# Another order of steps in the first stage of a transformer layer

## The chip, the cores and the metric

The kernel runs on one core of a Trainium2 chip, in one launch. The metric is the time of one execution on the device, in microseconds (us), lower is better. Five engines run at once, each through its own queue and strictly in that queue's order: TensorE (PE: matrix products; PEld is its weight load), VectorE (DVE), ScalarE (ACT), GpSimd (POOL) and SyncE (SP, which issues most transfers).

## The reference

One layer of an encoder in float32, for 256 tokens of width 2048. `c` is one vector that modulates all tokens.

```
c_act = silu(c)
mod = c_act @ mod_w + mod_b                        # 2048 -> 6 x 2048
sh_m, sc_m, g_m, sh_f, sc_f, g_f = split(mod, 6)
h = x * (1 + sc_m) + sh_m
q, k, v = split(h @ w_qkv + b_qkv)                 # 2048 -> 3072
q, k = rope(q), rope(k)                            # sin and cos of the positions
y = softmax with a sink(q k^T / 8, |q - k| <= 128) v @ w_o + b_o
x = layer_norm(alpha * x + (1 + g_m) * y)
h = x * (1 + sc_f) + sh_f
y = square(relu(h @ w1 + b1)) @ w2 + b2            # 2048 -> 8192 -> 2048
out = layer_norm(alpha * x + (1 + g_f) * y)
```

## The kernel before, in words

**Precision.** Each float32 operand of the large products is split into a high part (`hh`, `wh`) and a low part (`hl`, `wl`), and three TensorE products are summed: high by high (line 542), high by low (543), low by high (544). So each block of weights of 1 MB, once it has landed in a buffer `raw`, needs two casts on ScalarE (`wh`, line 281) and two subtractions on VectorE (`wl`, line 252, "lows" below).

**Stream.** All weights pass through one queue in a planned order (`S.plan`, `Stream`). A block is loaded as soon as one of the eight `raw` buffers of the first stage is free; a buffer comes free when the block's last reader has been recorded. `S.vecs(n)` performs the next n steps of modulation in that queue; the casts of the next block of weights can stand only behind the steps that are planned ahead of it.

**Modulation.** `mod` is cut by feature tiles k of 128 features (16 of them). For each k of the mixer's scale and shift there are two blocks of 1 MB. They are reduced either on TensorE (`Mod.step`, line 336, 32 pieces in the profile for one block, then the copy `mrow` at line 365 and a small product at line 416 that turns the row into columns), or on VectorE (`Col.step`, line 376, a product with `cb` summed along the row; `cb` is the activated vector spread over all partitions by `spread()`, line 137). `MIXP` says for each k which way: 1 is TensorE. `Group.columns` adds the bias, and `modulated(k)` makes `hh` (ScalarE, line 570) and `hl` (VectorE, lines 571 and 572) of the input tile.

**First stage.** The loop over n from 0 to 11 (line 650) takes one block of `wqkv` each, which holds four units (k, p): feature tile k against column part p of three. A unit is 12 matmuls: two token tiles by three products, each of them two. `AHEAD[n]` names the tiles whose blocks are planned behind block n and whose steps are made in its time; the strings `steps` give the order of units (`u`), steps of modulation (`g`) and `modulated` (`m`). TensorE's sums stay in six banks over all 12 blocks; the bias is added by line 197, the sums are copied out at line 581. `idle(n)` runs n products without use ahead of the first data. `bias_rows` prepares the bias, `rotary_tables` the sines and cosines, `masks` the window.

**After it.** The rest of the queries' and values' products runs between the attention of one group and the next (`SLOT_FILL` says how many steps of modulation are planned in each slot), then the output product, the first layer norm (`norm_scalars`, `normed`), and the MLP. The modulation ahead of the MLP comes in four groups of four tiles (`m_ff`): `FFP` says how many tiles of each group go to TensorE.

**Order.** What a scheduler does not pin stands where it puts it; casts, lows, `modulated` and the first product of a step of modulation keep the order of the program.

## Time and profile before

| | us |
|---|---|
| median of 3 runs (lowest, highest) | 1129.77 (1128.59, 1130.95) |
| profiled execution: time | 1130.56 |
| profiled execution: span of the core | 1128.8 |
| TensorE busy | 1072.6 |
| VectorE busy | 766.7 |
| ScalarE busy | 526.9 |

The profiled execution's time is 1.76 us more than the span, for what lies around it. Busy times are sums over the whole span; stages with different limits are mixed in them. PEclk in the views is the clock granted to TensorE as a share of full speed. In a row of the timeline the brackets hold the idle time of the engine ahead of that instruction and who ended it.

### The profile page before, as it was taken

The numbers are of one execution on the slowest core, as the hardware profiler recorded it, in microseconds if no ns is written. First come the engines' busy times: TensorE is split into PE (matmuls) and PEld (weight loads), VectorE is DVE, ScalarE is ACT, GpSimd is POOL, SyncE is SP. The second block draws the span as 40 slices with busy tenths as digits, with TensorE's granted clock in tenths as the row PEclk, the third lists the DMA queues.
The fourth block names the chain that finished last, engine by engine and source line by source line (L and its number), as shares of the span: only waits on it lengthen the run. The fifth ranks groups of instructions, "written<-read, shape, count | busy, mean of one in ns | idle before, by whom it ended". The sixth has DMA issues, their size and how long they took to land.

```text
span 1128.8 us, 16294 instructions
## 1 busy us (share of the span) xinstructions
PE 1072.6 (95%) x6563; PEld 887.9 (79%) x6563; DVE 766.7 (68%) x1103; ACT 526.9 (47%) x814; POOL 20.4 (2%) x40
## 2 busy tenths in 40 slices
PE   7778799999999699999999999999999999999995
PEld 6566577777778599998888888888888888888884
DVE  2656687877679866765568787865665656665576
ACT  3332357777753445653344443344444334444340
POOL 1000000000000000000000001000000000000001
PEclk9988899999999899999999999999999999999998
DMA  9989988877798878555587877776555555557521
GB/s 384 426 358 425 359 295 330 298 278 271 248 390 305 333 259 313 183 187 192 199 304 272 296 261 273 294 295 223 185 187 189 198 201 194 186 188 261 187 75 74
DMA packets 43653, 292.75 MB, mean 259 GB/s; under 512 B 4877, under 2 KB 5037, under 8 KB 9785
## 3 DMA queue, kind: packets, MB, share of 16 engines
q1 hardware_dynamic: 40400, 281.96, 67.7%
q0 software_dynamic: 2432, 8.41, 2.3%
q10 hardware_dynamic: 744, 1.34, 0.3%
q8 instruction: 51, 0.84, 0.3%
q14 instruction: 26, 0.20, 0.0%
HBM read 289.57 MB, written 2.11 MB: 258 GB/s over the span
## 4 chain that ended last, share of the span: by engine, by line
PE 86%; DVE 9%; ACT 3%; issue 1%; DMA 1%; DVEq 0%; ACTq 0%
PE pa L1046 16%; PE pa L543 15%; PE pa L544 15%; PE pa L542 15%; PE pa L1047 8%; DVE raw L376 4%; PE pm L336 4%; PE pa L1022 3%; PE pa L1023 3%; PE pa L1024 3%; DVE wl L252 3%; PE pa L715 1%; PE pt L754 1%; PE pa L770 1%; ACT wh L281 1%
## 5 line engine op out<-in xcount | busy, mean ns | idle before, releaser
L252 DVE TENSOR_TENSOR wl<-raw,wh 128x1024 fp32r<-128x1024 f32 x332 | 403.8, 1223 | 233.1 <-ACT wh L281 230.2
L281 ACT CAST wh<-raw 128x1024 fp32r<-128x1024 f32 x332 | 346.8, 1051 | 414.2 <-PE pa L544 214.6
L543 PE MATMUL pa<-wl,g 128*128 128x512 f32 x816 | 323.4, 396 | 22.0 <-DVE wl L252 21.9
L542 PE MATMUL pa<-wh,g 128*128 128x512 f32 x816 | 319.3, 397 | 4.9 <-ACT wh L281 4.0
L544 PE MATMUL pa<-wh,g 128*128 128x512 f32 x816 | 321.1, 394 | 0.0
L1046 PE MATMUL pa<-g,wh 128*128 128x512 f32 x768 | 271.6, 399 | 0.0
L1047 PE MATMUL pa<-g,wl 128*128 128x256 f32 x768 | 215.7, 281 | 0.0
L543 PEld LDWEIGHTS pa<-wl,g 128*128 128x128 f32 x816 | 155.3, 190 | 57.6 <-DVE wl L252 25.5
L542 PEld LDWEIGHTS pa<-wh,g 128*128 128x128 f32 x816 | 152.9, 188 | 45.1 <-issue 7.5
L544 PEld LDWEIGHTS pa<-wh,g 128*128 128x128 f32 x816 | 155.2, 190 | 33.0 <-issue 0.6
L1046 PEld LDWEIGHTS pa<-g,wh 128*128 128x128 f32 x768 | 144.3, 188 | 36.2 <-issue 0.2
L1047 PEld LDWEIGHTS pa<-g,wl 128*128 128x128 f32 x768 | 145.1, 189 | 0.1
L376 DVE CUSTOM_DVE_ANT_0 raw<-raw,cb 128x2048 f32<-128x2048 f32 x54 | 122.9, 2286 | 15.4 <-DMA raw<-in_mod 15.3
L1022 PE MATMUL pa<-g,wh 128*128 128x256 f32 x256 | 74.3, 290 | 0.3 <-ACT g L958 0.3
L1023 PE MATMUL pa<-g,wh 128*128 128x256 f32 x256 | 73.2, 287 | 0.0
L1024 PE MATMUL pa<-g,wl 128*128 128x256 f32 x256 | 72.8, 285 | 0.0
L1022 PEld LDWEIGHTS pa<-g,wh 128*128 128x128 f32 x256 | 49.8, 195 | 2.1 <-ACT g L958 1.1
L1023 PEld LDWEIGHTS pa<-g,wh 128*128 128x128 f32 x256 | 49.8, 195 | 0.4 <-issue 0.4
L1024 PEld LDWEIGHTS pa<-g,wl 128*128 128x128 f32 x256 | 49.7, 194 | 0.0
L336 PE MATMUL pm<-raw,cact 128*32 128x128 f32 (+1 forms) x1216 | 48.9, 305 | 0.0
L336 PEld LDWEIGHTS pm<-raw,cact 128*32 128x32 f32 x1216 | 34.2, 117 | 14.7 <-issue 12.1
L732 ACT ACTIVATE g<-g,nm 128x256 f32<-128x256 f32 x64 | 31.9, 500 | 18.6 <-DVE nm L722 18.6
(180 smaller groups left out, 659.0 us busy)
## 6 DMA issues: line engine op xcount, KB each, us to landing
raw<-in_mod SPq DMA_DIRECT2D x96, 1024.0 KB, 7.2
raw<-in_w SPq DMA_DIRECT2D x64, 1024.0 KB, 4.9
raw<-in_w1b SPq DMA_DIRECT2D x48, 1024.0 KB, 4.9
raw<-in_wqkv SPq DMA_DIRECT2D x24, 1024.0 KB, 7.1
raw<-in_wo SPq DMA_DIRECT2D x16, 1024.0 KB, 6.8
raw<-in_w1a SPq DMA_DIRECT2D x16, 1024.0 KB, 7.3
g<-in_x SPq DMA_DIRECT2D x4, 512.0 KB, 7.4
gb<-in_lnrow POOLq DMA_DIRECT2D x8, 256.0 KB, 6.0
```

Source lines behind the costliest of these rows:

```text
L252: self.pinned(nc.vector.tensor_sub(l, r, f32(self.hs[n])))
L281: self.pinned(nc.scalar.copy(h, s))
L336: i = nc.tensor.matmul(self.ps[32 * j:32 * j + 32, :w], lhsT[j] if type(lhsT) is list else lhsT, rhs[j], start=self.first, stop=stop)
L376: S.pinned(nc.vector.tensor_tensor_reduce(out=raw, in0=raw, in1=cb, scale=1.0, scalar=0.0, op0=OP.mult, op1=OP.add, accum_out=self.dst))
L542: nc.tensor.matmul(ps, xh, wh, start=start, stop=False)
L543: nc.tensor.matmul(ps, xh, wl, start=False, stop=False)
L544: S.prev = nc.tensor.matmul(ps, xl, wh, start=False, stop=stop).ins
L1022: nc.tensor.matmul(o, wh(w, 128), hh, start=new, stop=False)
L1023: nc.tensor.matmul(o, wh(w, 128), hl, start=False, stop=False)
L1024: nc.tensor.matmul(o, wl(w, 128), hh, start=False, stop=end)
L1046: nc.tensor.matmul(ps, wh(k, 128), hb, start=k == 0, stop=False)
L1047: nc.tensor.matmul(ps[:, :256], wl(k, 128), hb[:, :256], start=False, stop=k == NK - 1)
```

## The change

What it does, in the order of the program:

- The vector `c` gets a transfer of its own on SP (8 KB), and the packed constants move to ScalarE's queue, ahead of the first input tile.
- `spread()` and `bias_rows` move from ahead of the loop to behind its first turn; `idle(8)` becomes `idle(20)` ahead of the first step of modulation, and the five between the first two steps become six.
- `MIXP`: feature tiles 4, 8 and 12 go to VectorE and the other 13 to TensorE (before: 9 on TensorE, 7 on VectorE).
- `AHEAD` is written out by hand; tile 2 moves from the first turn to the second. In `steps` each `g` is now one block (before two), with units between; a tile that is left over at the end of a turn is modulated behind the first unit of the next (`owed`).
- `rotary_tables` becomes a generator: its five parts are made one per turn from n = 3 to 7 (before all in turn 2).
- `FFP`: the first MLP group goes to VectorE whole, the second to TensorE whole (before two tiles of each group to either). `columns` gets a form for four tiles.
- The activation `warm` (a square root without use) reads the last softmax sums in place of a constant.

```
-MIXP = tuple(int(k < 3 or k % 2 == 0) for k in range(16))
+MIXP = tuple(int(k not in (4, 8, 12)) for k in range(16))
-FFP = (2, 2, 2, 2)
+FFP = (0, 4, 2, 2)
...
+    cT = cst.tile([128, NK], F32, name="cT")
+    nc.sync.dma_start(cT, a["cT"])
     pack = cst.tile([128, 274], F32, name="pack")
-    nc.sync.dma_start(pack, a["pack"])
+    nc.scalar.dma_start(pack, a["pack"])
...
+            elif p == 2:
                 nc.tensor.transpose(pt[:, :128], r[:, :128], ident)
...
+            else:
+                for h in range(2):
+                    nc.tensor.transpose(pt[:, h * 128:h * 128 + 128], r[:, h * 128:h * 128 + 128], ident)
...
-    AHEAD, nm = [], 1
+    AHEAD = [[1], [2, 3], [4, 5], [6], [7], [8, 9], [10], [11], [12, 13], [14], [15], []]
...
     load_x(0)
-    bq = bias_rows(a["bqkv"], QKV)
-    spread()
-    idle(8)
     S.pin = True
+    idle(20)
     S.vecs(1)
-    idle(5)
+    idle(6)
     S.vecs(1)
     modulated(0)
     idle(6)
...
+    owed, tables = [], rotary_tables()
     for n in range(12):
         u, ms = units(n), list(AHEAD[n])
-        steps = "uuugmugm" if n == 0 else ["uuuu", "ugumuu", "ugumugum"][len(ms)]
-        for x in steps:
+        if n == 1:
+            steps = "ugugmugug"
+        else:
+            steps = ["uuuu", "ugugumu", "ugugumgug"][len(ms)]
+        for i, x in enumerate(steps):
             if x == "u":
                 next(u)
             elif x == "g":
-                S.vecs(2)
+                S.vecs(1)
             else:
                 modulated(ms.pop(0))
+            if i == 0 and owed:
+                modulated(owed.pop())
+        owed = ms
+        if n == 0:
+            spread()
+            bq = bias_rows(a["bqkv"], QKV)
         if n == 1:
             msk = masks()
-        if n == 2:
-            trig = rotary_tables()
+        if 3 <= n < 8:
+            next(tables)
...
-            warm = sml.tile([128, 1], F32, name="warm")
-            nc.scalar.activation(warm, eps, AF.Sqrt)
+            warm = sml.tile([128, 4], F32, name="warm")
+            nc.scalar.activation(warm, sums_of[0], AF.Sqrt)
```

**How the instructions move: the start on TensorE.** In the rows below, a line is one group of equal instructions in TensorE's queue; `identr` is the idle product, `raw,cact` a block of modulation, `ident,cact` the spreading of `cb`, `both,mrow` the turn of a row into columns. TensorE's first rows, before:

```order
L1213 UNCONDITIONAL_BRANCH
L137 MATMUL pa<-ident,cact 128x128 x16
L635 MATMUL pa<-identr 128x512 x8
L336 MATMUL pm<-raw,cact 32x128 x16
L635 MATMUL pa<-identr 128x512 x5
```

TensorE's first rows, now:

```order
L1236 UNCONDITIONAL_BRANCH
L647 MATMUL pa<-identr 128x512 x20
L343 MATMUL pm<-raw,cact 32x128 x16
L647 MATMUL pa<-identr 128x512 x6
L343 MATMUL pm<-raw,cact 32x128 x16
L423 MATMUL pt<-both,mrow 128x2
```

The 16 products that spread `cb` no longer stand at the head; they now stand in three groups around the last unit of the first turn and the first of the second.

**The middle of the first stage on VectorE.** `raw,cb` is a block of modulation on VectorE (tiles 7 before and 12 now), `wl<-raw,wh` a low. VectorE's rows, before:

```order
L376 ISA raw,modm<-raw,cb 128x2048
L376 ISA modm 128x1
L252 TENSOR_TENSOR wl<-raw,wh 128x1024
L410 TENSOR_TENSOR modm<-modm,pack 128x2
L571 TENSOR_SCALAR g_507<-g_507,modm 128x256
L572 TENSOR_TENSOR g_728<-g_507,g_727 128x256
```

VectorE's rows, now:

```order
L259 TENSOR_TENSOR wl<-raw,wh 128x1024 x2
L436 TENSOR_TENSOR modm<-pt,pack 128x2
L583 TENSOR_SCALAR g_562<-g_562,modm 128x256
L584 TENSOR_TENSOR g_777<-g_562,g_776 128x256
L259 TENSOR_TENSOR wl<-raw,wh 128x1024 x2
L383 ISA raw,modm<-raw,cb 128x2048
L383 ISA modm 128x1
```

A block on VectorE now stands behind both lows of the block of weights at hand, where before the lows stood behind the block. On ScalarE, in the same place, `g<-g,modm` is line 570 (now 582). Before:

```order
L365 COPY mrow<-pm 128x128
L570 ACTIVATE g_727<-g_507,modm 128x256
L281 CAST wh<-raw 128x1024 x2
L570 ACTIVATE g_727<-g_507,modm 128x256
L365 COPY mrow<-pm 128x128
```

ScalarE, now:

```order
L372 COPY mrow<-pm 128x128
L582 ACTIVATE g_776<-g_562,modm 128x256
L288 CAST wh<-raw 128x1024 x2
L372 COPY mrow<-pm 128x128
L582 ACTIVATE g_776<-g_562,modm 128x256
```

In most turns the two casts of the next block now stand right behind the modulation of a tile that came through TensorE.

**The first layer norm.** `sd` is the root of the variance of one of the two token tiles, `g<-g,nmr,r` the normalising of the second one. ScalarE, before:

```order
L789 ACT_TABLE_LOAD
L789 ACTIVATE sd<-ve 128x1
L281 CAST wh<-raw 128x1024
L789 ACTIVATE sd<-ve 128x1
L281 CAST wh<-raw 128x1024
L808 ACTIVATE g_2391<-g_2391,nmr,r_3360 128x512
```

ScalarE, now:

```order
L812 ACT_TABLE_LOAD
L812 ACTIVATE sd<-ve 128x1 x2
L288 CAST wh<-raw 128x1024 x2
L831 ACTIVATE g_2500<-g_2500,nmr,r_3448 128x512
L831 ACTIVATE g_2502<-g_2502,nmr,r_3448 128x512
```

VectorE at the same place, before (`qq` and `r` are steps of the reciprocal root):

```order
L794 TENSOR_SCALAR qq<-qq 128x1
L252 TENSOR_TENSOR wl<-raw,wh 128x1024
L795 TENSOR_TENSOR r_3360<-r_3360,qq 128x1
L252 TENSOR_TENSOR wl<-raw,wh 128x1024
L805 SCALAR_TENSOR_TENSOR nmr<-mv,r_3360 128x1
```

VectorE, now:

```order
L817 TENSOR_SCALAR qq<-qq 128x1
L833 TENSOR_SCALAR g_2506<-g_2506,mv,r_3407 128x512
L818 TENSOR_TENSOR r_3448<-r_3448,qq 128x1
L259 TENSOR_TENSOR wl<-raw,wh 128x1024
L828 SCALAR_TENSOR_TENSOR nmr<-mv,r_3448 128x1
L259 TENSOR_TENSOR wl<-raw,wh 128x1024
```

Both roots now stand ahead of the two casts; before one cast stood between them. Ahead of `nmr` stood two lows, now one.

More of the change, by code (lines that the diff above doesn't have):

```diff
@@ L101, in f32 @@
         return x.bitcast(F32)
+    cT = cst.tile([128, NK], F32, name="cT")
+    nc.sync.dma_start(cT, a["cT"])
     pack = cst.tile([128, 274], F32, name="pack")
-    nc.sync.dma_start(pack, a["pack"])
-    cT, b1 = pack[:, :NK], pack[:, NK:NK + 64]
+    nc.scalar.dma_start(pack, a["pack"])
+    b1 = pack[:, NK:NK + 64]
     modmb, modfb, gateb, lnT = (pack[:, 80 + 32 * n:112 + 32 * n].rearrange("p (n k) -> p n k", n=2)
@@ L148, in masks @@
         return msk
+    trig = cst.tile([128, 2, 3, NT, 32], F32, name="trig")
     def rotary_tables():
@@ L163, in rotary_tables @@
         nc.vector.tensor_scalar_add(kk, kk, -magic)
+        yield
         for cc in (c1, c2, c3):
@@ L167, in rotary_tables @@
         nc.vector.tensor_scalar(ang, ang, pi, -pi, op0=OP.min, op1=OP.max)
-        trig = cst.tile([128, 2, 3, NT, 32], F32, name="trig")
-        nc.scalar.activation(trig[:, 0, 2], ang, AF.Sin)
+        yield
         nc.vector.tensor_scalar_mul(nang, ang, -1.0)
@@ L173, in rotary_tables @@
         nc.vector.tensor_scalar_add(nang, nang, float(np.float32(math.pi / 2)))
+        yield
+        nc.scalar.activation(trig[:, 0, 2], ang, AF.Sin)
         nc.scalar.activation(trig[:, 0, 0], nang, AF.Sin)
+        yield
         nc.vector.tensor_scalar_mul(trig[:, 0, 1], trig[:, 0, 2], -1.0)
         nc.vector.tensor_scalar_mul(trig[:, 1], trig[:, 0], DH ** -0.5)
-        return trig
+        yield
     def bias_rows(src, n):
@@ L417, in columns @@
                 v = pt[:, :2].rearrange("p (n k) -> p n k", n=2)
-            else:
+            elif p == 2:
                 nc.tensor.transpose(pt[:, :128], r[:, :128], ident)
                 v = pt[:, :128].rearrange("p (n k q) -> p n k q", n=2, k=2)[:, :, :, 0]
+            else:
+                for h in range(2):
+                    nc.tensor.transpose(pt[:, h * 128:h * 128 + 128], r[:, h * 128:h * 128 + 128], ident)
+                v = pt[:, :256].rearrange("p (h j q) -> p j h q", h=2, j=4)[:, :, :, 0]
+                for n in range(2):
+                    d, b = (u[:, n, k0:k0 + 4].rearrange("p (j h) -> p j h", j=2) for u in (self.dst, self.mb))
+                    nc.vector.tensor_tensor(d, v[:, 2 * n:2 * n + 2], b, op=OP.add)
+                return
             nc.vector.tensor_tensor(self.dst[:, :, k0:k0 + p], v, self.mb[:, :, k0:k0 + p], op=OP.add)
@@ L483, in hybrid_kernel @@
         S.plan(a["wqkv"][n])
-        top = min((4 * n + 7) // 3, NK - 1)
-        AHEAD.append(list(range(nm, top + 1)))
-        for k in AHEAD[-1]:
+        for k in AHEAD[n]:
             if k in (2, 4, 8, 12):
@@ L489, in hybrid_kernel @@
             m_mix[k].plan(2)
-        nm = top + 1
     late = [m_gm] + m_ff[:3]
@@ L735, in scores @@
         PS[n] = P, sm, es
+    sums_of = []
     def normalise(n):
         P, sm, es = PS.pop(n)
+        sums_of[:] = [sm]
         rs = sml.tile([128, 4], F32, name="rs")
@@ L1195, in _layout @@
     o["lnrow"] = cc(np.stack([gm, bm, f(i["ln_mlp_g"])[0], f(i["ln_mlp_b"])[0]]))
-    flat = [o.pop(n).reshape(128, -1) for n in ("cT", "b1", "modmb", "modfb", "gateb", "lnT")]
+    flat = [o[n].reshape(128, -1) for n in ("cT", "b1", "modmb", "modfb", "gateb", "lnT")]
     snk = f(i["attn_sink"])[0].reshape(4, 2, 2, 2).transpose(0, 2, 1, 3).reshape(NH)
```

## The prediction

> **What bounds the kernel now.** I read the groups of instructions first, then the busy time of each engine by stage, then what TensorE waited for in the first stage.

> ```profile
> L252 DVE TENSOR_TENSOR wl<-raw,wh 128x1024 fp32r<-128x1024 f32 x332 | 403.8, 1223 | 233.1 <-ACT wh L281 230.2
> L376 DVE CUSTOM_DVE_ANT_0 raw<-raw,cb 128x2048 f32<-128x2048 f32 x54 | 122.9, 2286 | 15.4 <-DMA raw<-in_mod 15.3
> ```

> A low costs VectorE 1.22 us, and its idle time is spent on casts of ScalarE. A block of modulation on VectorE costs 2.29, nearly two lows. By stage (window, its length, then busy time of PE, PEld, DVE, ACT and POOL, then granted clock, DMA share, GB/s):

> ```profile
> 19.00:145.40 126.40, 99.75 (x824) 74.89 (x824) 77.13 (x112) 38.14 (x56) 0.00 (x0) 0.88 0.97 394
> 145.40:353.00 207.60, 205.42 (x1414) 152.86 (x1414) 163.74 (x317) 141.09 (x320) 3.87 (x7) 1.00 0.82 305
> 392.00:1128.80 736.80, 724.13 (x3997) 624.43 (x3997) 488.30 (x604) 326.04 (x412) 11.51 (x17) 0.99 0.62 219
> ```

> From 145.4 on TensorE is busy for 98% of these windows and has nothing to give. In the first stage 26.65 us of 126.4 are idle on TensorE, and the clock is 0.88. DMA is busy at 0.97, but only because `raw` buffers are refilled as they come free; who is waited for is told by TensorE's waits from 17 to 146 us (total, times, longest):

> ```profile
> PE pa L543 <- DVE wl L252: 21.1, 6, 5.8
> PE pa L542 <- ACT wh L281: 4.0, 3, 1.8
> PE pt L416 <- ACT mrow L365: 1.4, 3, 0.5
> PE pa L542 <- ACT g L570: 0.9, 1, 0.9
> ```

> Six waits for lows carry 21.1 us. One of them, and what follows a short idle time on the clock:

> ```profile
> 68.83 0.80 PE L543 MATMUL pa<-wl,g 128*128 128x512 f32 x1 [5.82 <-DVE wl L252]
> ```

> ```profile
> 34.00:38.00 4.00, 4.00 (x12) 3.05 (x12) 4.00 (x5) 2.05 (x3) 0.00 (x0) 0.57 1.01 428
> ```

> The lows of those blocks stand in VectorE's queue behind one or two blocks of modulation. The first stage is thus bounded by VectorE's order, not by VectorE's total (77 of 126 us) nor by the transfers.

> **The change part by part: TensorE's start.** The rows of before from the first instruction to the first main product, and VectorE's bias casts:

> ```profile
> 4.67 6.51 PE L137 MATMUL pa<-ident,cact 128*128 128x128 f32 x32 [4.67 <-ACT cact L126]
> 10.93 2.09 PE L635 MATMUL pa<-identr 128*128 128x512 f32 x8
> 12.96 1.08 PE L336 MATMUL pm<-raw,cact 128*32 128x128 f32 x32
> 19.06 1.68 PE L542 MATMUL pa<-wh,g 128*128 128x512 f32 x6 [0.35 <-ACT wh L281]
> ```

> ```profile
> 7.50 0.43 DVE L192 CAST g<-g 128x512 fp32r<-128x512 f32 x1 [1.77 <-DMA g<-in_bqkv]
> 8.09 0.68 DVE L193 TENSOR_TENSOR g<-g,g 6x512 fp32r<-6x512 f32 x1
> ```

> The spreading (6.51) and eight idle products (2.09) go from the head; 20 idle products take their place. At 0.26 each (2.09/8) they take 5.2 us, at twice that 10.4; begun at about 4.67 they end between 9.9 and 15.1. Before, the first block began at 12.96. I take no change there, since the idle products are likely half cold, half warm. Behind it one more idle product: +0.23. The first main product then starts at 19.06 + 0.23 = 19.3 (bounds 17 and 21.4). The transfer of `c` on its own is small and ahead of all else on SP; `pack` is first needed by the bias behind the first small product, some 4 us after the first block: nothing, bounds -0.5 to +0.5, in the range.

> **TensorE's work in the stage.** The pace, from the chain that ended last and the timeline in the middle of the stage:

> ```profile
> 20.97 0.23 PE pa L544
> 30.73 0.27 ACT mrow L365
> 31.05 0.40 PE pt L416 x2
> 31.66 0.60 ACT g L570
> 32.26 0.94 ACT wh L281
> 33.23 0.98 DVE wl L252
> ```

> ```profile
> 111.90 1.08 PE L336 MATMUL pm<-raw,cact 128*32 128x128 f32 x32
> 112.91 0.50 PE L543 MATMUL pa<-wl,g 128*128 128x512 f32 x1
> 113.24 0.40 PE L544 MATMUL pa<-wh,g 128*128 128x512 f32 x1
> 113.48 0.32 PE L416 MATMUL pt<-both,mrow 128*128 128x2 f32 x2
> 115.62 0.80 PE L542 MATMUL pa<-wh,g 128*128 128x512 f32 x2 [1.82 <-ACT wh L281]
> 144.84 0.61 PE L197 MATMUL pa<-g,g 128*128 128x512 f32 x2
> 145.39 1.07 PE L336 MATMUL pm<-raw,cact 128*32 128x256 f32 x16
> ```

> The stage ends for me where the first block of the next modulation starts: 145.39. A product costs 0.2275 (0.23 in the chain), so 288 of them (12 blocks x 24) 65.5; six bias products at 0.23 are 1.4. A block of modulation costs 1.01 (111.90 to 112.91) and makes the next product 0.10 longer: 1.1. Behind the first main product stood 16 such blocks, now 24 (tiles 1 to 15 without 4, 8 and 12, two each): 26.4 instead of 17.6. The turn into columns costs 0.35, now 12 times: 4.2 instead of 2.8. The spreading, warm now, takes half of its 6.51: 3.2. Together 100.7, so that without any wait the stage would end at 19.3 + 100.7 = 120.0.

> **The waits that remain.** VectorE's blocks fall from 14 to 6 in this stage, which is 8 x 2.29 = 18.3 us off VectorE, and they stand behind the lows. I let the 21.1 us go. What is late next is ScalarE: the casts of the next block of weights stand in its queue behind the `modulated` of a tile, and this behind the whole chain of a block of TensorE's modulation: copy, small product, bias, `hh`, cast. From 113.48 to 115.62 that chain shows: 2.14 less 0.35 for the columns and 3 x 0.23 for the products that could stand there is 1.1, and I take 1.2 for a turn (bounds 0, where the casts come free early, and the whole 1.82 of the row). Turns 3 to 10 have it: 8 x 1.2 = 9.6. The table parts on VectorE and their table load on ScalarE fall into five of these turns:

> ```profile
> 64.50 0.38 DVE L157 TENSOR_SCALAR g<-pack,posf 128x32 f32<-128x32 f32 x2
> 67.56 3.49 DVE L252 TENSOR_TENSOR wl<-raw,wh 128x1024 fp32r<-128x1024 f32 x3
> 63.69 1.28 ACT L170 ACT_TABLE_LOAD   x1
> ```

> They take 3.06 us of VectorE (64.50 to 67.56) and 1.28 of ScalarE; of 4.3 at the most and nothing at the least I take 2.5, as two of the five parts stand in front of a waiting chain. Turn 0: the first low against the first product of its kind, 0.7 (bounds 0 and 1.2). Turn 1 carries the tile that was begun in it, with the bias now in front of its lows: copy 0.45 (1.4/3), the chain to `hh` 0.9, and on VectorE 0.43 + 0.68 + 1.22 = 2.3, in all 3.6 (bounds 1.3, where the bias lies beside the spreading, and 3.6). Turn 2: copy 0.4, a low 0.7, and 0.6 for tile 4's sums on VectorE, 1.7 (bounds 0.4 and 3.5, a block and a low). The sum is 0.7 + 3.6 + 1.7 + 9.6 + 2.5 = 18.1, and the end 138.1.

> **The clock.** From 31.45, when the small product of the chain above had ended (31.05 + 0.40), to 33.20, when the cast had (32.26 + 0.94), TensorE was idle, 1.75 us; in the window 34 to 38 the clock was 0.57. This short wait lost 4 x 0.43 = 1.7 us. The waits at turn 1 and at turns 4 and 5 are longer than that, so three drops are 5.1; other idle times of the same length left the clock alone (1.82 us before 115.62, with products at 0.40 after), so I take half: 2.5, bounds 0 and, with a drop at each of ten turns, 17. The stage ends at 140.6: 4.8 us gained.

> [...]

> **Behind the stage.** Two places more:

> ```profile
> 150.74 0.50 PE L543 MATMUL pa<-wl,g 128*128 128x512 f32 x1 [0.86 <-DVE wl L252]
> ```

> ```profile
> 378.52 6.04 DMA raw<-in_w1a
> 384.64 1.04 ACT wh L281
> 388.28 1.14 DVE wl L252
> 389.52 2.23 ACT g L808 x3
> ```

> The wait of 0.86 is that of the first block of queries on VectorE, which has no tile of the mixer behind it any more: +0.9 (bounds 0 and 0.9). At the layer norm the second `sd` stood behind a cast that waited for `w1a` until 384.6, and `nmr` behind two lows that followed from it; then came the normalising from 389.52. Now both roots are made ahead of the casts, and one low stands ahead of `nmr`. The earliest end of that low is 384.64 + 1.04 + 1.14 = 386.8; with 0.3 for `nmr` and the queue the normalising starts at 387.1: 2.4 gained (bounds 0, where the transfer comes later or the tail fills with other work, and 3.1, where that low comes later still). `warm` moves a table load and leaves their number: 0 (bounds -1.28 and +1.28).

> `FFP`: TensorE's blocks of the MLP's modulation are eight tiles before and after, 0. VectorE's first group grows by two tiles, four blocks of 2.29 us earlier, in the stretch 145 to 353, where it is busy for 164 of 208 us; the cover is its 44 idle us. Without the cover these are 9.2 us, of which two blocks could reach TensorE before the second group, now wholly on TensorE, pays it back: I take -1.0 (bounds 0 and -4).

> **The sum.** 4.8 + 0.9 + 2.4 - 1.0 = 7.1. The span of 1128.8 becomes 1121.7, the profiled execution's time with 1.76 around it 1123.5; that execution stood 0.79 above the median (1130.56 against 1129.77), so the median should be 1122.7.

> **The rivals.** No change of the clock: as the sum, with the term of 2.5 left out, 1120.2. For it speaks the 1.82 us that left the products at 0.40; against it 34 to 38.

> Pace of the transfers: the casts come free early enough in every turn and the clock holds. The gain is 7.1 + 9.6 + 2.5 = 19.2, the time 1110.6. The floor below that is the landing of the last `wqkv` block: 12 + 32 blocks and 2 MB of input at 428 GB/s are 112.7 us, from 4.67 on 117.4, and a cast, a low and 24 products later about 125, 1107. Against it: ScalarE's order puts the casts behind the tile in most turns.

> The waits only change their place: each of the eight turns costs the 1.82 us of the row instead of 1.2, 5 us more, and VectorE gives back another 1: gain 1.1, time 1128.7. It has for it that the same chain did cost 1.82 where it stood in before.

> Slower through the clock: half-speed stretches behind the turns. A drop costs 1.7 us, and 1.5 of them are in the sum; 7.1/1.7 = 4.2 more, near six in all, bring the time back to that of before, and from seven on the kernel is slower. With one at each of ten turns: 14.5 more, 1137.2. For it: idle 1.2 to 2.6 us recurs at every turn, where before long stretches lay between; against it: 113.48 to 115.62.

> That the change doesn't do what it says can be for `warm` alone, and costs nothing.

> **How the numbers follow.** The chances: the sum 0.42 (1120 to 1127), the clock holding 0.10, the pace of the transfers 0.16 (1107 to 1117), waits that change their place 0.20 (1127.5 to 1132), the clock at every turn 0.12 (above 1132). Less than 0.2%, or 2.3 us, can't be told from no change. Faster is 0.42 + 0.10 + 0.16 = 0.68, the same 0.20, slower 0.12. From 1114 to 1131 leaves about 0.08 of the fast case and 0.12 above. The likeliest alone is good for 1120 to 1127: two thirds of the bounds on its terms.

> **What the next profile would show.** Waits of TensorE for lows between 17 and 146 us fall from 21.1 to about 5, waits for `wh` rise from 4.0 to about 10 in eight to ten pieces; the first block of the next modulation stands at about 140.6; VectorE's busy time in the stage falls by 18; no wait at the first block of queries; both `sd` ahead of the casts and the normalising of the second token tile at about 2.4 us less behind the landing of `w1a`; the clock below 0.7 in two or three places only. I am wrong if the casts wait twice as long, if the clock falls at each turn, or if VectorE's early MLP blocks hold lows in 145 to 353.

## The result and the profile after

The changed kernel took 1122.65 us (median; 1121.65 to 1123.10) beside 1129.42 for the kernel before it on the same chip: a ratio of 0.9937, 95% interval 0.9920 to 0.9954, so 5.2 to 9.0 us faster. The forecast was 1122.7. The number was met; its terms were off by some 2 to 3 us on either side and cancelled, as the experiments show. One execution of e8 below took 2168.43 us at a granted clock of 1.00; its cause is not known, and its row leaves it out.

The profiled execution of the changed kernel has a span of 1119.9. By stage, in the same columns as before (the first stage, the stretch to the norm, the MLP):

```profile
17.70:141.60 123.90, 108.50 (x1118) 79.14 (x1118) 61.10 (x100) 40.07 (x63) 0.00 (x0) 0.99 1.01 408
141.60:349.20 207.60, 205.66 (x1295) 152.00 (x1295) 163.38 (x318) 145.15 (x325) 3.86 (x7) 1.00 0.82 309
384.70:1119.90 735.20, 722.78 (x4000) 623.32 (x3998) 488.10 (x605) 326.75 (x413) 11.48 (x17) 0.99 0.62 221
```

In the first stage TensorE's idle time fell from 26.65 to 15.4 us, its clock rose from 0.88 to 0.99, and its work rose: 108.5 us busy for 99.75, although the busy time of before is stretched by half clock. VectorE's fell by 16. TensorE's waits from 17 to 146 us:

```profile
PE pa L554 <- ACT wh L288: 7.0, 10, 1.0
PE pa L555 <- DVE wl L259: 4.8, 4, 2.0
PE pt L423 <- ACT mrow L372: 2.9, 6, 0.7
PE pa L554 <- ACT g L582: 0.9, 1, 0.9
```

Waits for lows fell from 21.1 to 4.8, waits for casts rose from 4.0 to 7.0 in ten pieces. Rows of the timeline of TensorE through the stage (start, length, and in brackets the idle time ahead):

```profile
17.75 0.73 PE L554 MATMUL pa<-wh,g 128*128 128x512 f32 x2 [0.34 <-ACT wh L288]
22.40 0.40 PE L556 MATMUL pa<-wh,g 128*128 128x512 f32 x1
22.73 1.08 PE L343 MATMUL pm<-raw,cact 128*32 128x128 f32 x32
23.74 0.50 PE L554 MATMUL pa<-wh,g 128*128 128x512 f32 x1
24.07 0.40 PE L555 MATMUL pa<-wl,g 128*128 128x512 f32 x1
...
40.62 0.79 PE L555 MATMUL pa<-wl,g 128*128 128x512 f32 x1 [2.01 <-DVE wl L259]
...
96.61 1.68 PE L554 MATMUL pa<-wh,g 128*128 128x512 f32 x6 [1.02 <-ACT wh L288]
...
134.54 1.67 PE L554 MATMUL pa<-wh,g 128*128 128x512 f32 x6 [1.02 <-ACT wh L288]
141.62 1.07 PE L343 MATMUL pm<-raw,cact 128*32 128x256 f32 x16
```

The first main product starts at 17.75 (19.06 before), the stage ends at 141.62 (145.39 before). The turn waits are the predicted ones, a cast behind the activation of a tile: four are of 1.02 to 1.04, the other six of 0.33 to 0.56.

The norm, in the chain of the changed kernel:

```profile
362.28 7.86 DMA raw<-in_w1a
...
375.05 2.20 DVE raw L383
...
381.28 1.14 DVE wl L259
...
382.53 0.82 ACT g L831
383.39 1.54 PE pt L975 x6
384.95 0.58 PE pa L1045
```

The transfer is no longer late. What is late next is VectorE: a block of modulation (375.05) stands ahead of the second tile's statistics. From the last blocks of modulation (377.93 before, 372.17 now) to the first product of the MLP (392.25, 384.95) the norm took 14.32 us before and 12.78 now.

### The profile page after: what moved, and what is told of

It reads as the page before. It is cut to its first block, busy times and chain, and to the rows that moved or that the text cites. A ratio compares the mean times of both kernels' runs of the same rounds, so it can differ in the third digit from the quotient of the medians.

```text
span 1119.9 us, 16590 instructions
## 1 busy us (share of the span) xinstructions
PE 1077.6 (96%) x6712; PEld 886.7 (79%) x6712; DVE 747.6 (67%) x1086; ACT 527.0 (47%) x817; POOL 20.4 (2%) x40
## 4 chain that ended last, share of the span: by engine, by line
PE 89%; DVE 6%; ACT 2%; DMA 2%; issue 1%; DVEq 0%; ACTq 0%; SPq 0%
PE pa L1069 16%; PE pa L554 16%; PE pa L555 16%; PE pa L556 15%; PE pa L1070 8%; PE pm L343 4%; PE pa L1045 3%; PE pa L1046 3%; PE pa L1047 3%; DVE wl L259 2%; PE pa L735 1%; PE pa L793 1%; PE pt L777 1%; ACT wh L288 1%; DVE raw L383 1%
## 5 line engine op out<-in xcount | busy, mean ns | idle before, releaser
L383 DVE CUSTOM_DVE_ANT_0 raw<-raw,cb 128x2048 f32<-128x2048 f32 x46 | 104.8, 2283 | 8.5 <-DMA raw<-in_mod 8.3
L343 PE MATMUL pm<-raw,cact 128*32 128x128 f32 (+1 forms) x1344 | 54.6, 301 | 0.0
```

Source lines behind the costliest of these rows:

```text
L343: i = nc.tensor.matmul(self.ps[32 * j:32 * j + 32, :w], lhsT[j] if type(lhsT) is list else lhsT, rhs[j], start=self.first, stop=stop)
L383: S.pinned(nc.vector.tensor_tensor_reduce(out=raw, in0=raw, in1=cb, scale=1.0, scalar=0.0, op0=OP.mult, op1=OP.add, accum_out=self.dst))
```

## The experiments

All were compared with the kernel before on their own chip. The stage's end is the start of the first block of the next modulation; "half clock" counts stretches of 3.41 us with a granted clock of 0.50 in the stage, in the profiled execution.

| kernel | median us | ratio to before (95%) | stage end | half clock |
|---|---|---|---|---|
| before | 1129.4 to 1130.5 | 1 | 145.39 | 9 |
| changed | 1122.65 | 0.9937 (0.9920 to 0.9954) | 141.62 | 1 |
| e1 casts first | 1122.40 | 0.9939 (0.9927 to 0.9952) | 140.37 | 3 |
| e2 start of before | 1115.81 | 0.9876 (0.9861 to 0.9891) | 135.90 | 1 |
| e3 MLP groups of before | 1131.00 | 1.0014 (1.0005 to 1.0023) | 143.22 | 3 |
| e4 tiles of before | 1138.10 | 1.0071 (1.0058 to 1.0084) | 158.06 | 9 |
| e5 norm's waits filled | 1119.57 | 0.9908 (0.9893 to 0.9923) | 143.41 | 3 |
| e6 before, new tiles alone | 1120.66 | 0.9914 (0.9901 to 0.9926) | 133.25 | 3 |
| e7 first stage alone | 1127.46 | 0.9972 (0.9963 to 0.9982) | 143.69 | 3 |
| e8 e2 and e5 | 1113.18 | 0.9855 (0.9842 to 0.9869) | 134.29 | 0 |
| e9 old order and start | 1113.44 | 0.9849 (0.9836 to 0.9863) | 132.26 | 2 |
| e10 e9 and norm filled | 1112.61 | 0.9833 (0.9819 to 0.9847) | 131.95 | 2 |
| e11 tables whole | 1124.30 | 0.9945 (0.9932 to 0.9957) | 143.44 | 3 |
| e12 spreading at the head | 1122.92 | 0.9931 (0.9919 to 0.9944) | 143.66 | 4 |

**Table of tiles and order (e4, e6).**

```
e4, in the changed kernel:
-MIXP = tuple(int(k not in (4, 8, 12)) for k in range(16))
+MIXP = tuple(int(k < 3 or k % 2 == 0) for k in range(16))
e6: the reverse, in the kernel before
```

> The changed kernel with seven tiles of the mixer on VectorE, as before the change, in the new order of steps. Theory A (the blocks on VectorE hold the lows): TensorE has 8.8 us less to do (8 blocks at 1.1), but waits for lows rise from 4.8 to 15 to 22 us: the stage ends 2 to 8 us later, time 1124.5 to 1130.5. Theory B (the order of single blocks with units between is what takes the waits away): waits for lows stay below 8 us, the stage ends 3 to 6 us earlier, time 1117 to 1120.

> The kernel before with only the table of tiles changed: 4, 8 and 12 on VectorE, the other 13 on TensorE; order, start and MLP as before. Theory A (fewer blocks on VectorE are what helps): waits for lows fall from 21.1 us to below 8, half clock in the stage from nine windows to four or fewer, TensorE works 10 us more: the stage ends at 138 to 143, the time is 1122 to 1127. Theory B (table and order help only together): pairs of blocks in a row keep 8 to 15 us of waits, the stage ends at 145 to 153, time 1129 to 1137.

The new table alone, in the old order, is 9.2 us faster (1120.66), more than the whole change brought: theory A of e6, and beyond its numbers. The old table in the new order is 8 slower than before (1138.1): e4's theory A, beyond its range too. Of the stage's ends, table by order: 145.39 and 133.25 in the old order (old and new table), 158.06 and 141.62 in the new one. In this stage the table is worth 12 to 16 us; the rest of the change, the new order and start, costs 8 to 13 with either table. The two largest groups of TensorE's waits in the stage, e4 (17 to 158 us) and e6 (17 to 146 us):

```profile
PE pa L555 <- DVE wl L259: 17.2, 6, 5.0
PE pa L554 <- ACT wh L288: 13.0, 10, 3.6
```

```profile
PE pa L543 <- DVE wl L252: 5.8, 1, 5.8
PE pa L542 <- ACT wh L281: 3.8, 5, 1.8
```

In e6 five of the six long waits for lows are gone. The one that is left (at 65.71) is behind the tables of sines, which the old order makes whole in one turn: VectorE works on them from 61.46 to 64.3, and the low begins at 64.44.

**The start (e2, e12).**

```
e2:      load_x(0)
+    bq = bias_rows(a["bqkv"], QKV)
+    spread()
+    idle(8)
     S.pin = True
-    idle(20)
...
-            spread()
-            bq = bias_rows(a["bqkv"], QKV)
e12: as e2, but bias_rows stays behind the first turn
```

> The changed kernel with the spreading of cb, the bias rows and eight idle products at the head again, as before the change. Theory A (order at turn 1): the start is 1.3 us later, the spreading (3.7 us with the longer products behind it) leaves the stage, and the wait of 2.01 us for a low at 40.6 and the half clock behind it (1.4 us) go: stage end 5 to 6 us earlier, time 1116.5 to 1118. Theory B (pace of the transfers): the block of turn 2 lands no sooner than 47.7 us, so all but 1 to 2 us of this turns into waits for it, and the late start costs 1.3: time 1121.5 to 1124.

> The changed kernel with the spreading of cb and eight idle products at the head as before, the bias rows left behind the first turn. Theory A (the spreading costs 3.7 us of TensorE in the stage, the bias rows a wait of 2.0 and a window of half clock): 3 to 4 us faster than the changed kernel, 1118.5 to 1119.7, and the wait of 2.0 us at turn 1 is still there. Theory B (one of them carries all 6.8 us): 1115.5 to 1116.5 without that wait, or 1122 to 1123.5.

e2 is 6.8 us faster than the changed kernel and ends its stage at 135.90, 5.7 earlier: theory A, the time 0.7 beyond its range (the first main product is not later than the changed kernel's: 17.28). e12 gains nothing and grows the wait at turn 1; its theory A fell. The chain of e12 and the row on TensorE that it leads to:

```profile
34.82 4.99 DMA g<-in_bqkv
39.92 0.44 DVE g L199
40.38 0.68 DVE g L200
41.08 1.24 DVE wl L259
```

```profile
42.36 0.80 PE L555 MATMUL pa<-wl,g 128*128 128x512 f32 x1 [6.26 <-DVE wl L259]
```

The bias rows' own two transfers are issued from ScalarE's queue, from 34.25 on there, and have landed at 39.8; VectorE's cast of the first stands ahead of the lows. In the changed kernel they are issued at 31.0, ahead of ScalarE's copy for the next tile and not behind it, and VectorE has no wait for them. So the moved bias rows carry a loss of their own, and its size differs with the time of their issue. With both at the head it is gone; the bias rows alone at the head were not run.

**The groups of the MLP (e3, e7).**

```
e3:  -FFP = (0, 4, 2, 2)
     +FFP = (2, 2, 2, 2)
e7: as e3, and warm is a root of a constant again
```

> The changed kernel with two tiles of each group of the MLP's modulation on TensorE, as before the change. Theory A (the early VectorE blocks are covered): the time is within 0.8 us of the changed kernel, and the stretch from the first stage's end to the last block of modulation ahead of the norm is as long, 230.5. Theory B (the prediction's price of 1.0 with a bound of 4): it is 1 to 4 us faster in that stretch. Theory C: this part is what made the stretch 2.0 us shorter and the norm's waits 1.5 us shorter; then 2 to 3.5 us slower.

> The changed kernel with the groups of the MLP's modulation and the early square root as before the change; what is left of the change is the first stage alone. Theory A (in the kernel with only the groups undone the wait of 1.6 us in the last softmax and its 1.7 us of half clock come from the two table loads that the moved square root brings there): no such wait, 3 to 3.5 us less than that kernel's 1131.0: 1127.5 to 1128.5. Theory B (it comes from the order of the groups' blocks): 1130 to 1132.

e3 is 8.4 us slower than the changed kernel, more than any theory had. The profiled spans (1129.2 and 1119.9) split it: 1.6 in the stage, whose order is the same (three half-clock stretches for one), 4.95 from the stage's end to the last blocks (235.50 for 230.55), 0.96 in the norm (13.74 for 12.78), 1.8 behind it. Timeline of TensorE, the second group's blocks in the changed kernel and in e3:

```profile
297.68 1.93 PE L343 MATMUL pm<-raw,cact 128*32 128x256 f32 x32
299.54 1.09 PE L777 MATMUL pt<-ident,g 128*128 128x128 f32 x8
```

```profile
303.68 1.08 PE L343 MATMUL pm<-raw,cact 128*32 128x128 f32 x32
304.69 0.55 PE L777 MATMUL pt<-ident,g 128*128 128x128 f32 x3
...
324.55 2.53 PE L777 MATMUL pt<-ident,g 128*128 128x128 f32 x8 [1.59 <-ACT g L767]
```

With the group whole on TensorE two blocks stand in a row and take 1.86 together, one change-over for two (a change-over is what a block costs TensorE beyond its own 1.01 us when large products stand around it, 0.2 in the first stage); without it they stand singly at 1.01 with a change-over each. And e3 has a wait of 1.59 behind the last softmax, with half clock behind it. e7 takes back the moved square root as well, and that wait is gone with 3.5 us: theory A there. So the moved root, with its two table loads in the softmax (1.28 us each, at 315.22 and 316.74 in e3), costs in the old grouping and is hidden in the new one. What is left of the change in e7, the first stage alone, is worth 2.4 us by the medians and 3.2 by the ratio (0.9972); groups and root together are worth the other 4.8 (1127.46 to 1122.65), or 4.0 by the ratios.

e7 has no such wait, and its stretch up to the last blocks takes 231.65 us, 1.1 more than the changed kernel's, with the same one wait of 1.8 in both: that is what the groups' blocks cost TensorE more when they stand singly. The larger part lies at the norm. In e3 and e7 the order there is the old one, with two lows ahead of `nmr` and a cast between the two roots, and this cast waits for its transfer. ScalarE in e7:

```profile
381.69 1.05 ACT L288 CAST wh<-raw 128x1024 fp32r<-128x1024 f32 x1 [4.33 <-DMA raw<-in_w1a]
```

The norm takes 13.96 us in e7, and 737.1 follow behind it. So the new order at the norm, which the prediction counted apart from the groups, comes with them.

**The norm's waits and the clock (e5, e8).**

```
     S.vecs(4)
+    idle(16)
...
+                    if (g, kp, i, t) == (0, 0, 0, 1):
+                        idle(10)
```

> The changed kernel with 16 products without use on TensorE ahead of the first layer norm's transposes and 10 more ahead of those of the second token tile; they fill waits of 4.7 and 3.1 us. Theory A (the clock is granted by how much of a window of some 3.4 us TensorE worked; the waits in the norm cost half clock behind it): the clock stays at 1.00 from 375 to 390 us, the products of the MLP behind the norm take 0.12 us from the first on, 1.5 to 2 us faster than the changed kernel: 1120.5 to 1121.3. Theory B (the half clock there has another cause, or the idle products delay the transposes): 0 to 3 us slower, 1122.5 to 1125.5.

> The changed kernel with the start of before (spreading, bias rows, eight idle products at the head) and with the idle products in the norm's waits. Theory A (both effects add): 1115.8 less 1.7, 1113.6 to 1114.8. Theory B (the idle products gain nothing): 1115.5 to 1118.5.

Theory A both times, a little beyond its range (0.9 and 0.4). The window that it speaks of is 3.41 us long in the profiles (last section). The windows behind the norm, of the changed kernel and of e5:

```profile
385.00:390.00 5.00, 5.00 (x47) 3.70 (x48) 2.52 (x9) 3.89 (x9) 0.00 (x0) 0.65 1.01 424
```

```profile
375.00:385.00 10.00, 9.67 (x103) 7.19 (x94) 9.03 (x25) 4.49 (x8) 0.00 (x0) 1.00 0.90 353
385.00:390.00 5.00, 5.00 (x58) 4.24 (x59) 3.42 (x12) 4.72 (x9) 0.00 (x0) 1.00 1.02 416
```

From the first product of the MLP to the end the changed kernel takes 735.0 us, e5 733.4 (1118.4 less 384.99): 1.6, as expected. The kernel before took 736.6 there, since its longer wait was followed by more half clock:

```profile
392.30:399.30 7.00, 7.00 (x48) 5.09 (x49) 3.85 (x7) 3.80 (x7) 0.00 (x0) 0.50 0.63 227
```

**ScalarE's order (e1).**

```
-            steps = ["uuuu", "ugugumu", "ugugumgug"][len(ms)]
+            steps = ["uuuu", "uguguum" if n else "ugugumu", "ugugumgug"][len(ms)]
```

> The changed kernel, but from turn 1 on a turn with one tile makes this tile behind its last unit and not ahead of it, so that ScalarE's two casts of the next block of weights stand ahead of the tile's activation. Theory A (ScalarE's order): the six waits of 1.02 to 1.04 us, and those of 0.33 to 0.56, on the cast at a turn go, with some 0.15 each that the first product behind a wait takes longer: the stage ends 5 to 7 us earlier (at about 136), the time is 1115.5 to 1118. Theory B (pace of the transfers; DMA moves 408 GB/s in the stage and is never free): the casts then wait for their block, the stage ends 0 to 2 us earlier, the time is 1120.5 to 1123.

The time is the changed kernel's, so theory A fell as a forecast of time. (The expectation miscounts: the changed kernel has four waits of 1.02 to 1.04, not six.) TensorE's waits in its stage (17 to 141 us):

```profile
PE pa L555 <- DVE wl L259: 7.3, 9, 2.0
PE pt L423 <- ACT mrow L372: 2.6, 6, 0.4
PE pa L554 <- ACT wh L288: 2.6, 5, 0.6
```

The waits for casts did go, from 7.0 to 2.6; but 2.5 came back as waits for the lows of the same blocks, and two more stretches of half clock fell into its stage and one behind it (at 212). Theory B had the time right, but not the reason: no wait on a transfer stands in these rows, and no cast or low of this stage waits for one either.

**Order, tables and transfers (e9, e10, e11).**

```
e9: the changed kernel with start, AHEAD and steps of before (S.vecs(2) for a g)
e10: e9 with the idle products of e5
e11: -        if 3 <= n < 8:
     -            next(tables)
     +        if n == 2:
     +            for _ in tables: pass
```

> The changed kernel with the start, the order of steps (two blocks in a row for one g) and the order of tiles of before; what stays of the change is the table of tiles, the groups of the MLP, the early square root and the tables of sines in five parts. Theory A (single blocks between units cost TensorE two change-overs for one, and the tables made whole are the one wait of 5.8 us that is left in the old order): no wait above 2 us in the stage, its end at 126 to 129, the time 1106.5 to 1110.5. Theory B (pace of the transfers bounds the stage at about 130 to 133): 1112 to 1116.

> The kernel of the run before it, with the idle products in the norm's waits. Theory A: 2 to 3 us less than that kernel. Theory B (it is bound elsewhere): the same within 1 us.

> The changed kernel with the tables of sines and cosines made whole behind turn 2, as before the change. Theory A (3.1 us of VectorE and the table load stand in one piece ahead of the lows of a block): a wait of 4 to 6 us for a low at about 66 us with one or two windows of half clock, the wait of 1.7 at 75 gone: 3 to 7 us slower than the changed kernel, 1125.5 to 1129.5. Theory B (the parts only spread the same delay over five turns, as the prediction's 2.5 us supposes): within 1.5 us of it.

e9 came out in theory B's numbers, 9.2 us faster than the changed kernel (9.9 by the ratios), but for the most part not for B's reason: of TensorE's waits one of 0.4 is on a transfer, and one more, of 1.66 at 106.44, is for a cast that itself waited 1.00 for its block.

```profile
PE pa L557 <- ACT wh L288: 4.9, 5, 1.8
PE pt L423 <- ACT mrow L372: 2.9, 6, 0.7
PE pa L558 <- DVE wl L259: 1.7, 1, 1.7
PE pa L557 <- ACT g L585: 0.9, 1, 0.9
PE pm L343 <- DMA raw<-in_mod: 0.4, 1, 0.4
```

Its stage is 114.9 us long with these 10.8 of waits: it is bound mostly by TensorE's work. The windows of this stage in e9 and in e2, which has the new order with the old start:

```profile
17.40:132.30 114.90, 103.94 (x1090) 77.52 (x1092) 59.83 (x96) 37.15 (x58) 0.00 (x0) 0.97 1.01 420
```

```profile
17.30:135.90 118.60, 104.05 (x1086) 75.65 (x1087) 60.06 (x98) 36.96 (x58) 0.00 (x0) 0.99 1.01 420
```

The busy times are alike, but e9 has two stretches of half clock in it and e2 one; at 1.7 each, e9 has some 1.8 less of TensorE's work, which its pairs of blocks may save (not shown apart), and loses as much to the clock. The 3.7 us between the two stages are waits: TensorE is idle for 14.55 us in e2 and 10.96 in e9. e11 is 1.7 us slower than the changed kernel by the medians and 0.9 by the ratios, with intervals that overlap, so it can't be told from it, which is nearer to its theory B. In its profile the wait of 2.9 on a cast and two more stretches of half clock are partly paid back by turn waits of 0.34 in place of 1.02 in the turns behind. e10, the fastest, can't be told from e9: behind the norm it took 733.4 us for e9's 735.5, but its profiled execution has two stretches of half clock at 202.7, which e9's has not.

## Why the prediction was right

In sum it was right by 0.1 us. Point by point:

- **Lows.** That five of their six waits come from VectorE's blocks is shown by e6, and that the casts come next by the rows after: 7.0 in ten pieces, forecast "about 10 in eight to ten". The row that I showed for it, at 68.83, is the sixth: 3.06 us of tables stand ahead of that low, and the wait stays in e6. The turn wait of 1.2 measured 1.02 to 1.04 in four turns and 0.33 to 0.56 in six.
- **The start.** Forecast 19.3, measured 17.75, within its bounds. The idle products begin at 4.11 and the first block at 11.42, 1.5 earlier than I had let it be. That the 20 would go half at one pace and half at the other is what the trace shows: they start 0.43 us apart up to 9.40 and 0.23 apart from 9.73 on, 7.31 in all, though the views give a clock of 1.00 over both. Since e2 with the idle products of before starts at 17.28, this is not won by the moved spreading. In the kernel before, the spreading waits for `cact` and this for the packed constants (landed at 4.3) and begins at 4.67; in e2, with a transfer of its own for `c`, it begins at 3.32. So the transfer that I put at nothing brings some 1.35 of these 1.8.
- **Turn 1.** Forecast 3.6 (0.45 + 0.9 + 2.3), measured 0.44 + 0.89 + 2.01. The mechanism was incomplete: I counted VectorE's instructions on the bias and not its transfer, whose issue moved with it. In the changed kernel it lands in time; in e12 VectorE waits 4.17 for it.
- **TensorE's work.** 100.7 was too little. One block costs 1.21 with its change-overs (from 22.40 + 0.23 to 24.07, less a product of 0.23), not 1.1, which is 2.2 for the 20 blocks that stand singly. In all the stage held 123.9 - 15.4 - 1.7 = 106.8 of work; of the other 3.9 the spreading is 0.2 (3.42 for 3.2, from the starts of its three groups to the products behind them), and the rest was not taken apart. The products of the spreading start 0.11 us apart in this stage; at the head of the kernel before they start 0.21 apart up to 10.35 and 0.11 behind it. The term for the waits, 18.1, was too large against 15.4 idle. So the stage ended at 141.62 for a forecast of 140.6.
- **The clock.** One stretch of half clock, 1.7, for a forecast of 2.5: near, but halved for a wrong reason. I read that the wait of 1.82 before 115.62 left the clock alone, since the products behind it took 0.40. Both start ahead of 116.14, and from there on the kernel before runs at half clock:

```profile
112.73:116.14 3.41, 1.59 (x18) 0.89 (x6) 1.60 (x4) 2.37 (x4) 0.00 (x0) 1.00 1.01 428
116.14:119.56 3.42, 0.28 (x1) 0.00 (x0) 3.42 (x3) 0.38 (x1) 0.00 (x0) 0.50 0.96 362
```

- **Behind the stage.** Forecast +0.9, +2.4 and -1.0. The wait of 0.86 did go. The norm gained 1.54, and what is late next there is not only the low that I named but a block of modulation on VectorE ahead of it. The step that failed is the price of the groups: I costed them at nothing on TensorE and a loss on VectorE. Together with the root they brought 4.0 to 4.8 us. In the profiles of e7 and the changed kernel this is 1.1 through pairs of blocks, 1.2 in the norm, whose new order comes with the groups, and 2.1 behind it, where half clock lasts 3.5 us and not 8.5, a term that the sum did not have.
- **What cancelled.** The first stage alone brought 2.4 us in the medians (e7; 3.2 by the ratio), where 4.8 + 0.9 were forecast; the rest brought 4.8 (4.0) where 1.4 was. That the total came within 0.1 us is luck, and no proof of its terms.
- **The rivals.** Pace of the transfers is not what bounds the stage: in e9, whose stage is 9 us shorter, waits on them are single ones. No turn wait on a cast reached the 1.82 of the rival in which waits only change their place. The half clock at every turn did not come, and the clock did not hold throughout either.

## What to carry to other kernels

Where a change has several parts, time each in the old surroundings before the parts are packed together: here the table alone gave 9 us in the old order, and the new order and start took some 8 back in the same stage. A moved setup step takes its transfer with it, so look where in its queue that is issued (e12). Two blocks of modulation in a row cost TensorE less here than two single ones (1.86 for 2.02, and one change-over fewer). And filling waits that can't be removed with products without use took 1.6 us off the stretch behind the norm (e5); in e10 the gain was not clear of the noise.

## What the runs showed of the clock

```profile
36.92:40.33 3.41, 1.20 (x4) 0.67 (x4) 2.85 (x5) 1.38 (x2) 0.00 (x0) 1.00 1.02 423
40.33:43.75 3.42, 3.13 (x28) 2.21 (x32) 0.23 (x1) 0.00 (x0) 0.00 (x0) 0.50 1.01 422
43.75:47.16 3.41, 2.97 (x54) 1.99 (x46) 0.00 (x0) 0.68 (x2) 0.00 (x0) 1.00 0.98 387
```

```profile
198.93:202.34 3.41, 1.84 (x20) 0.79 (x18) 3.21 (x5) 2.73 (x6) 0.00 (x0) 1.00 0.55 223
202.34:209.17 6.83, 5.47 (x40) 3.90 (x41) 6.58 (x12) 4.15 (x9) 0.00 (x0) 1.00 0.98 337
```

```profile
199.27:202.68 3.41, 1.18 (x17) 0.42 (x16) 3.41 (x5) 2.73 (x7) 0.00 (x0) 1.00 0.62 219
202.68:209.51 6.83, 6.12 (x28) 3.90 (x30) 4.64 (x7) 2.83 (x6) 0.00 (x0) 0.50 0.95 361
```

A window in which TensorE was busy for 1.2 us is followed by half clock, one with 1.84 is not. On the grids of all 14 profiles, from 15 to 400 us, every window at full clock with under 1.6 us of work was followed by half clock, and none with over 2.1; between them it went both ways (1.62 us and full clock behind it in e4, 2.08 and half clock in e7). So a wait of 1.8 us is dear or free by where it falls on the grid: e9 and e10 have the same wait of 2.9 us on a copy at this place, and only in e10 does enough of it lie in one window. This also sets how far the profile of one execution can be compared with another: kernels with the same order in the stage (changed, e3, e5, e7) have one to three such stretches there, and their stage ends lie 2 us apart.
